# Linear attention in seven steps per head pair, and three modulation parts moved from the first layer's mixer to its MLP

## The chip, the cores and the metric

The kernel runs on one core of a Trainium2 chip. The metric is the device time of one execution in microseconds (us), as the median of several runs. TensorE multiplies matrices, VectorE and ScalarE do elementwise work, GpSimd some subtractions and clears, and SyncE issues most transfers.

## The reference

Two layers of a transformer-like block run over 512 latent and 256 context tokens of width 1024, all in float32. Every layer derives six modulation rows per stream, latent and context, from a conditioning vector:

```
mod_l = split(silu(c)     @ ada_w[layer] + ada_b[layer], 6)     # ada_w: 1024 x 6144
mod_c = split(silu(c_ctx) @ ada_w[layer] + ada_b[layer], 6)
u   = rmsnorm(x, g0) * (1 + mod[1]) + mod[0]
x   = x + mod[2] * rmsnorm(mix(u) @ w_out, g1)
x   = x + mod[5] * rmsnorm(relu(h @ w1)**2 @ w2, g3),   h = rmsnorm(x, g2) * (1 + mod[4]) + mod[3]
```

"Part (layer, i)" below is mod[i] of that layer. The mixer of layer 0 is a gated linear attention (8 heads, chunks of 64 tokens, forward and backward) beside a grouped-query softmax attention with rotary positions. The mixer of layer 1 is an mLSTM beside a retention. Only the latent stream leaves layer 1, so its parts 2 to 5 are wanted for the latent stream alone; all other parts are wanted for both streams.

## The kernel before, in words

Large float32 products are split into a rounded high and a low half (`split`, lines 196 to 198: ScalarE rounds, VectorE subtracts) and run as three matmuls (`mm3`, lines 488 to 490). The stages follow one another: startup with the first projection; the linear-attention stage; the softmax attention; the output projection; the first MLP; layer 1's mixer; its output projection; the second MLP.

**Order.** Within a stage Python generators cut the work into steps, and the strings of `PLAN` (line 133) say in which program order steps are taken. The framework puts in all semaphores, and its scheduler places the instructions on each engine by program order and its own estimates of when each can start. So a plan gives priority and the order in which buffers are handed out; a step's instructions can stand on an engine among those of other steps. On the engine itself, and in SyncE's queue, they run in order.

**Linear-attention stage** (`gla`, lines 805 to 963; driven at lines 1202 to 1208). One generator goes through the four head pairs one after the other, four steps a pair ("G", sixteen in all). A pair: gate products (L846), three ScalarE functions (L849 to L851), L852 on VectorE, cumulative sums on TensorE (L858), exponentials (L865), products with q and k (L874), transposes (L879), copies (L884, L886); then decays (L893) and chunk states (L908), their copies (L913), two scans (L919, L922); then scores (L935), mask (L938 to L944) and outputs (L954, L957); then a head norm. Its tiles E, Ei, Ek, lg, As and the scan's X have one buffer each. Among these steps stand "q", one token tile of the attention's query projection (24 matmuls, then rotary work that "l" advances), and "a", one step of `ada_steps` (lines 247 to 264). A step "a" loads two weight tiles of 128x1024 (512 KB) from `ada_w` and multiplies them, in fp32, with the conditioning of both streams on 32 columns: four 512-column products for two parts at once. Eight steps make a pair of parts, and `ada_finish` adds the bias and writes the rows to DRAM. The stage makes (0,2) with (0,3), (0,4) with (0,5), and (1,0) with (1,1): 24 steps, 48 tiles.

**The first MLP** (`mlp`, lines 585 to 792) goes through eight blocks of 512 hidden columns. A block has four hidden steps ("h") and seven products ("P") of one block against the hidden steps of the next. The sub-matrices of the second weight are subtracted on GpSimd (L638), and results are added into the sum on VectorE (L744). Every W1 and `ada_w` tile comes through one ring of three buffers (tag `raw`). Beside that "s" advances a side generator, `ada_part` (lines 293 to 317). It makes one part without matmuls: per step one 512 KB tile comes in, and VectorE multiplies its two halves by the conditioning and adds them up (L310 for the first half of a sum, L312 for the others), for the latent stream alone. After eight steps two fp32 products with a matrix of ones (L315) sum over the partitions, and `ada_rows` (lines 319 to 335) clears a tile on GpSimd (L324, L325), fetches the bias and writes the row out (L332, L333). The side generator makes (1,2) to (1,5) in the first MLP.

Of the kernel before, what the change touches and what calls it, by code (L numbers as in the profile page):

```python
# [8 lines left out]
F32 = mybir.dt.float32  # L9
# [3 lines left out]
ALU = mybir.AluOpType  # L13
# [109 lines left out]
def const_offsets():  # L123
# [11 lines left out]
    "gla": "GaGaGaqGaalGaaGalaqaaaGaGGlGlaaaqGaaaGaGlGlaqGGaaa",  # L135
    "att": "QQSSSSQSSSfSVSfSSSVSfSSSVfQSSSVSSVSSSVfQfVSSVVSfVSVQSSVSSVfVSVSSVSVSSVSVSVMSVSMVVSSVSSSVVSVMVVVVVVVM",
# [3 lines left out]
    "mlp": ["sPhPPshPPhsPPhsP", "PhPPhPPhPPhP"],  # L140
# [4 lines left out]
class Kern:  # L145
# [147 lines left out]
    def ada_part(self, layer, part, pool):  # L293

        nc = self.nc
        W = self.a["ada_w"][layer]
        c0 = part * 1024
        md = self.T(self.dram, [1, 1024])
        acc = [self.T(pool, [128, 512], F32, tag="sp", bufs=2) for _ in range(2)]
        for x in range(2):  # L300
            for kk in range(4):
# [4 lines left out]
                for k in range(2):  # L306
                    w = raw[:, k * 512:(k + 1) * 512]
                    c = self.sT[:, 2 * kk + k, 0:1]
                    if kk == 0 and k == 0:
                        nc.vector.tensor_scalar(out=acc[x], in0=w, scalar1=c, scalar2=None, op0=ALU.mult)  # L310
                    else:
                        nc.vector.scalar_tensor_tensor(out=acc[x], in0=w, scalar=c, in1=acc[x], op0=ALU.mult, op1=ALU.add)  # L312
        ps = self.pb()
        for x in range(2):
            nc.tensor.matmul(ps[32 * x:32 * x + 32, :], self.ones, acc[x], start=True, stop=True)  # L315
        self.ada_rows(layer, part, ps, [(0, 0), (512, 0)], md)
# [488 lines left out]
    def gla(self, ga, gqk, gv, lr, done):  # L805

        nc, C = self.nc, self.C0
        mm = nc.tensor.matmul
# [28 lines left out]
        nc.scalar.copy(lrT, pt[:, :768])  # L837

        X, XC = self.T(ga, [128, 708]), self.T(ga, [128, 256])
        nc.gpsimd.memset(X, 0.0)  # L840
        nc.gpsimd.memset(XC, 0.0)
        xc = XC.rearrange("p (e c) -> p e c", c=4)
        for p in range(4):
# [67 lines left out]
            for b in range(2):  # L911
                n = 6 - b
                nc.scalar.copy(U[:, :704].rearrange("p (e s) -> p s e", s=11)[:, b::2],  # L913
                               pu[:, b * 512:b * 512 + n * 64].rearrange("p (s e) -> p s e", s=n))

            for d in range(2):
# [27 lines left out]
            nc.vector.tensor_tensor(out=Av, in0=Av, in1=C["diag2"].unsqueeze(1).to_broadcast([128, 12, 64]), op=ALU.mult)  # L944
            po = self.pa()
# [211 lines left out]
    def layer0(self):  # L1157
# [6 lines left out]
        with self.pool("mx") as mx:  # L1164
# [11 lines left out]
            with self.pool("ga") as ga:  # L1176
# [21 lines left out]
                def ev2(t, ps):  # L1198
# [3 lines left out]
                ada = (x for layer, parts in ((0, (2, 3)), (0, (4, 5)), (1, (0, 1))) for x in self.ada_steps(layer, parts, self.po()))  # L1202
                gla = self.gla(ga, [gqk[:, p] for p in range(4)], [gv[:, p] for p in range(4)], lr,
                               lambda p: nc.sync.dma_start(out=on_d[p * 128:(p + 1) * 128, :], in_=gqk[:, p]))
                ops = {"G": lambda: next(gla), "q": lambda: next(qsteps), "a": lambda: next(ada, None), "l": later}
# [47 lines left out]
        with self.pool("xw", bufs=3) as xw, self.pool("h0") as h0:  # L1253
# [3 lines left out]
            with self.pool("p5") as p5, self.pool("ya") as yap:  # L1257
# [427 lines left out]
    def layer1(self):  # L1685
# [101 lines left out]
        with self.pool("xw1", bufs=3) as xw, self.pool("h1") as h1, self.pool("p7") as p7:  # L1787
# [20 lines left out]
            self.mlp(1, uT3, 512, (self.r2, self.r2), h1, acc, xw, ([(0, 256), (256, 512)], [(0, 512)]), done)  # L1808
# [42 lines left out]
```

## Time and profile before

| | |
|---|---|
| median of 3 runs | 1749.84 us (1747.56 to 1750.02) |
| the profiled execution | 1746.07 us |
| its span, first to last instruction | 1744.4 us |
| TensorE, VectorE, ScalarE, GpSimd busy | 95%, 65%, 45%, 15% |
| granted TensorE clock, mean | 0.981 of full speed |

The linear-attention stage lies at about 125 to 275 us of the span, the softmax attention up to 435, the output projection up to 522, the first MLP with its epilogue up to 1050, and the second MLP's steady part at 1430 to 1680. A row `L312 DVE ...` is line 312 of the kernel on VectorE (PE is TensorE, ACT ScalarE, POOL GpSimd, SPq SyncE's queue). All tiles have the name `x`.

### The profile page before, as it was taken

What the parts mean: (1) busy time and instruction counts of PE and PEld (TensorE: products, weight loads), DVE (VectorE), ACT (ScalarE), POOL (GpSimd) and SP (SyncE); (2) the same over time, 40 slices, a digit from 0 to 9 for tenths busy, and PEclk for the clock granted to TensorE, in tenths of its full rate; (3) what the DMA queues carried; (4) which work ended last, traced back from release to release, by engine and by line L of the source; (5) the groups of instructions that cost most, each with busy time, mean ns of one, the idle gap of its engine ahead of it and who ended that gap; (6) DMA issues with size and microseconds to landing.
All of it is one profiled execution on the core that took longest, in us unless ns stands there. A gap on an engine that the chain in (4) does not pass through costs nothing.

```text
span 1744.4 us, 25127 instructions
## 1 busy us (share of the span) xinstructions
PE 1660.3 (95%) x9795; PEld 1316.5 (75%) x9795; DVE 1131.3 (65%) x1678; ACT 791.5 (45%) x1392; POOL 264.3 (15%) x216
## 2 busy tenths in 40 slices
PE   7998999999999999999999999978998999999998
PEld 5775555755778888888888878757887788888876
DVE  5435456465678558657668693466786676777876
ACT  5335435464345434334333454635552355445443
POOL 0000020100002211121120000164011112223210
PEclk9999999999999999999999999988996999999999
DMA  9415666231654224224123552234545533333322
GB/s 289 129 52 178 202 205 223 72 91 37 205 169 128 90 61 155 74 83 157 62 90 118 176 192 64 84 104 130 161 132 164 181 98 108 110 108 99 107 86 84
DMA packets 174746, 220.67 MB, mean 127 GB/s; under 512 B 17450, under 2 KB 112742, under 8 KB 174628
## 3 DMA queue, kind: packets, MB, share of 16 engines
q1 hardware_dynamic: 169444, 201.24, 36.7%
q0 software_dynamic: 5184, 17.83, 3.0%
q8 instruction: 77, 1.26, 0.3%
q14 instruction: 41, 0.34, 0.1%
HBM read 193.74 MB, written 25.30 MB: 126 GB/s over the span
## 4 chain that ended last, share of the span: by engine, by line
PE 77%; DVE 9%; DMA 6%; ACT 4%; issue 3%; SPq 1%; POOL 0%; DVEq 0%; ACTq 0%; POOLq 0%
PE x L488 21%; PE x L489 21%; PE x L490 21%; DMA x<-in_ada_w_dram 2%; PE x L1116 2%; PE x L260 2%; DVE x L198 2%; PE x L1107 1%; PE x L1093 1%; DMA x<-x 1%; ACT x L197 1%; PE x L1542 1%; PE x L957 1%; PE x L435 1%; PE x L1681 1%
## 5 line engine op out<-in xcount | busy, mean ns | idle before, releaser
L488 PE MATMUL x<-x,x 128*128 128x512 f32 (+2 forms) x2042 | 763.3, 375 | 12.1 <-ACT x L197 3.4
L489 PE MATMUL x<-x,x 128*128 128x512 f32 (+2 forms) x2050 | 762.8, 373 | 7.1 <-DVE x L198 7.1
L490 PE MATMUL x<-x,x 128*128 128x512 f32 (+2 forms) x2050 | 761.1, 372 | 0.1
L198 DVE TENSOR_TENSOR x<-x,x 128x1024 fp32r<-128x1024 f32 (+4 forms) x373 | 395.5, 1079 | 216.5 <-ACT x L197 211.4
L197 ACT CAST x<-x 128x1024 fp32r<-128x1024 f32 (+4 forms) x373 | 332.7, 911 | 388.4 <-PE x L489 181.3
L488 PEld LDWEIGHTS x<-x,x 128*128 128x128 f32 x2042 | 387.4, 190 | 91.1 <-ACT x L197 9.0
L489 PEld LDWEIGHTS x<-x,x 128*128 128x128 f32 x2050 | 389.1, 190 | 75.7 <-DVE x L198 11.7
L490 PEld LDWEIGHTS x<-x,x 128*128 128x128 f32 x2050 | 388.9, 190 | 70.6 <-issue 6.3
L638 POOL TENSOR_TENSOR x<-x,x 128x1024 f32<-128x1024 f32 x56 | 145.5, 2599 | 546.3 <-DMA x<-in_mlp_w_dram 250.2
L744 DVE TENSOR_TENSOR x<-x,x 128x512 f32<-128x512 f32 x225 | 143.9, 680 | 12.3 <-PE x L490 11.2
L689 ACT ACTIVATE x<-x 128x512 f32<-128x512 f32 (+4 forms) x96 | 44.3, 477 | 91.2 <-PE x L490 91.2
L312 DVE SCALAR_TENSOR_TENSOR x<-x,x,x 128x512 f32<-128x512 f32 x56 | 53.1, 948 | 20.8 <-DMA x<-in_ada_w_dram 19.9
L260 PE MATMUL x<-x,x 128*32 128x512 f32 x192 | 45.6, 604 | 7.5 <-DMA x<-in_ada_w_dram 7.4
L690 ACT ACTIVATE x<-x 128x512 f32<-128x512 f32 (+4 forms) x96 | 48.0, 516 | 2.1
L1095 DVE TENSOR_REDUCE x<-x 128x1 f32<-128x768 f32 (+1 forms) x48 | 36.6, 775 | 18.9 <-PE x L1093 18.7
L1116 PE MATMUL x<-x,x 128*64 128x512 f32 x112 | 44.2, 618 | 1.0 <-ACT x L1110 0.7
L1096 ACT ACTIVATE x<-x,x 128x768 f32<-128x768 f32 (+1 forms) x48 | 36.3, 757 | 12.5 <-DVE x L1095 12.3
L1107 PEld LDWEIGHTS x<-x,x 128*128 128x128 f32 x224 | 24.5, 141 | 22.9 <-issue 21.1
L675 DVE TENSOR_TENSOR x<-x 128x768 f32<-128x768 f32 (+1 forms) x28 | 38.4, 1371 | 0.0
L1093 PE MATMUL x<-x,x 128*128 128x256 f32 (+1 forms) x160 | 36.7, 347 | 1.3 <-ACT x L1096 1.3
L799 DVE TENSOR_REDUCE x<-x 128x8 f32<-128x512 f32 (+1 forms) x19 | 14.3, 753 | 35.5 <-ACT x L797 35.4
L797 ACT ACTIVATE x<-x 128x512 f32<-128x512 f32 (+1 forms) x19 | 12.8, 673 | 47.6 <-PE x L957 25.8
(316 smaller groups left out, 1517.8 us busy)
## 6 DMA issues: line engine op xcount, KB each, us to landing
x<-in_mlp_w_dram SPq DMA_DIRECT2D x128, 512.0 KB
x<-in_ada_w_dram SPq DMA_DIRECT2D x96, 512.0 KB
x<-x SPq DMA_DIRECT2D x42, 512.0 KB
x<-x SPq DMA_DIRECT2D x50, 256.0 KB
x<-in_cd_w_in_dram SPq DMA_DIRECT2D x24, 512.0 KB
x<-x POOLq DMA_DIRECT2D x36, 256.0 KB, 3.1
x<-in_ab_w_in_dram SPq DMA_DIRECT2D x16, 512.0 KB
x<-x SPq DMA_DIRECT2D x20, 384.0 KB
```

Source lines behind the costliest of these rows:

```text
L197: self.nc.scalar.copy(hi, src)
L198: self.nc.vector.tensor_tensor(out=lo, in0=src, in1=hi.bitcast(F32), op=ALU.subtract)
L260: nc.tensor.matmul(ps[32 * g:32 * g + 32, :n], self.sT[:, k, :], rs[g], start=k == 0, stop=k == 7)
L312: nc.vector.scalar_tensor_tensor(out=acc[x], in0=w, scalar=c, in1=acc[x], op0=ALU.mult, op1=ALU.add)
L488: mm(out, st[0], mv[0], start=start, stop=False, skip_group_check=partial)
L489: mm(out, st[0], mv[1], start=False, stop=False, skip_group_check=partial)
L490: mm(out, st[1], mv[0], start=False, stop=stop, skip_group_check=partial)
L638: sub = lambda out, x, y: nc.gpsimd.tensor_tensor(out=out, in0=x, in1=y, op=ALU.subtract)
L690: nc.scalar.activation(out=hh[:, f, c0:c1], in_=h[:, c0:c1], func=AF.Square)
L744: nc.vector.tensor_tensor(out=dst, in0=dst, in1=acc[j], op=ALU.add)
L1093: mm(pS[:, s0:s1], qs[:, h * 128:(h + 1) * 128], kst[kv][i][:, s0:s1], start=i == 0, stop=i == 1)
L1116: mm(po[64 * kv:64 * kv + 64, :], av[:, kt * 128 + kv * 64:kt * 128 + kv * 64 + 64], PT[kv], start=kt == 0, stop=kt == nk - 1)
```

## The change

- **Linear attention.** The set-up common to all pairs becomes `gla_setup`. `gla` takes one pair `p`, and has three more yields (after the products with q and k, after the chunk states' copies, after the mask): seven steps a pair. Four generators stand side by side as "0" to "3" in the plan, which takes the later steps of one pair among the first of the next. X and XC become tiles with one buffer that each pair takes anew; only XC is still cleared.
- **Query tiles.** The plan of this stage takes all six "q" (four before) and twelve "l". One fill step "f" of the attention's plan stands elsewhere.
- **Modulation.** The stage keeps (0,2) with (0,3), and (0,4) alone: sixteen "a". With one part a step loads one tile and has four products of 256 columns.
- **The first MLP** makes (0,5), (1,0), (1,1), then (1,2), (1,3), (1,4). `ada_part` now makes a part for both streams (`ns` = 2) unless it is one of layer 1's later parts: four VectorE operations a tile, and a set of ones products and of rows for each half of 512 columns. The plan has six "s" a block (four before).
- **The second MLP** gets a side generator too, for (1,5), with two "s" a block; its ones and sums lie in the ring `t4` of seven tiles.

```
-    "gla": "GaGaGaqGaalGaaGalaqaaaGaGGlGlaaaqGaaaGaGlGlaqGGaaa",
+    "gla": "0a0q0l0a1la0q0l1a0l1aq1l2a1l1aq2l1a2l2a3ql2a2l3a2q3la3l3a3a3aa",
-    "mlp": ["sPhPPshPPhsPPhsP", "PhPPhPPhPPhP"],
+    "mlp": ["PshsPPshPPhssPPhsP", "PhPPshPPhPPhsP"],
...
-    def ada_part(self, layer, part, pool):
+    def ada_part(self, layer, part, new):
...
-        acc = [self.T(pool, [128, 512], F32, tag="sp", bufs=2) for _ in range(2)]
+        ns = 1 if layer == 1 and part > 1 else 2
+        md = self.T(self.dram, [2, 1024])
+        held = []
         for x in range(2):
+            acc = [new() for _ in range(ns)]
+            held += [(j, x, acc[j]) for j in range(ns)]
             for kk in range(4):
                 raw = self.T(self.w1, [128, 1024], F32, tag="raw", bufs=3)
...
                 yield
                 for k in range(2):
                     w = raw[:, k * 512:(k + 1) * 512]
-                    c = self.sT[:, 2 * kk + k, 0:1]
+                    for j in range(ns):
+                        c = self.sT[:, 2 * kk + k, j:j + 1]
+                        if kk == 0 and k == 0:
+                            nc.vector.tensor_scalar(out=acc[j], in0=w, scalar1=c, scalar2=None, op0=ALU.mult)
+                        else:
+                            nc.vector.scalar_tensor_tensor(out=acc[j], in0=w, scalar=c, in1=acc[j], op0=ALU.mult, op1=ALU.add)
+            if len(held) == 2:
+                ps = self.pb()
+                for i, (_, _, r) in enumerate(held):
+                    nc.tensor.matmul(ps[32 * i:32 * i + 32, :], self.ones, r, start=True, stop=True)
+                self.ada_rows(layer, part, ps, [(y * 512, j) for j, y, _ in held], md)
+                held = []
...
-    def gla(self, ga, gqk, gv, lr, done):
+    def gla_setup(self, ga, lr):
...
+        return wgr, lrT
+
+    def gla(self, ga, p, gqk, gv, sets, done):
...
+            yield
...
+            yield
+
+            X, XC = self.T(ga, [128, 708], tag="X", bufs=1), self.T(ga, [128, 256], tag="XC", bufs=1)
+            nc.gpsimd.memset(XC, 0.0)
...
+            yield
...
-                ada = (x for layer, parts in ((0, (2, 3)), (0, (4, 5)), (1, (0, 1))) for x in self.ada_steps(layer, parts, self.po()))
+                ada = (x for layer, parts in ((0, (2, 3)), (0, (4,))) for x in self.ada_steps(layer, parts, self.po()))
+                pair = [self.gla(ga, p, ...) for p in range(4)]
...
-                    for part in range(2, 6):
-                        yield from self.ada_part(1, part, p5)
+                    for layer, part in ((0, 5), (1, 0), (1, 1), (1, 2), (1, 3), (1, 4)):
+                        yield from self.ada_part(layer, part, lambda: self.T(p5, [128, 512], F32, tag="sp", bufs=2))
...
+            t4 = lambda: self.T(p7, [128, 1024], F32, tag="t4", bufs=7)
+            self.ones = t4()[:, :32]
+            self.mlp(1, ..., done, self.ada_part(1, 5, lambda: t4()[:, :512]))
```

## Rows read from the trace of the kernel before

**Rows 1.** The page: busy time and share by engine; the chain by engine.

```profile
PE 1660.3 (95%) x9795; PEld 1316.5 (75%) x9795; DVE 1131.3 (65%) x1678; ACT 791.5 (45%) x1392; POOL 264.3 (15%) x216
...
PE 77%; DVE 9%; DMA 6%; ACT 4%; issue 3%; SPq 1%; POOL 0%; DVEq 0%; ACTq 0%; POOLq 0%
```

**Rows 2.** Stretches of the span: busy us (instructions), granted clock, DMA share, GB/s.

```profile
core 0: us, PE busy (x) PEld busy (x) DVE busy (x) ACT busy (x) POOL busy (x), PEclk, DMA share, GB/s
124.90:275.00 150.10, 132.54 (x1765) 76.26 (x1764) 72.81 (x120) 66.67 (x117) 15.71 (x19) 0.99 0.61 200
275.00:435.00 160.00, 157.12 (x777) 99.67 (x776) 95.99 (x147) 87.85 (x185) 10.78 (x12) 1.00 0.28 92
522.00:541.00 19.00, 19.00 (x125) 17.37 (x124) 18.17 (x12) 8.53 (x13) 11.23 (x4) 1.00 0.47 140
522.00:780.00 258.00, 258.00 (x1351) 221.14 (x1350) 172.50 (x195) 110.00 (x164) 51.45 (x23) 1.00 0.32 97
780.00:985.00 205.00, 203.60 (x1041) 172.57 (x1039) 141.79 (x177) 76.98 (x108) 25.00 (x13) 1.00 0.38 120
985.00:1050.00 65.00, 63.03 (x295) 50.91 (x296) 59.67 (x130) 33.91 (x83) 2.21 (x4) 1.00 0.50 170
1430.00:1680.00 250.00, 249.41 (x1099) 205.70 (x1098) 188.99 (x218) 126.95 (x182) 62.92 (x24) 1.00 0.33 100
```

**Rows 3.** Groups by line, whole trace: busy us, mean ns | idle before, releasers.

```profile
L260 PE MATMUL x<-x,x 128*32 128x512 f32 x192 | 45.6, 604 | 7.5 <-DMA x<-in_ada_w_dram 7.4
...
L385 PE MATMUL x<-x,x 128*32 128x256 f32 x128 | 8.6, 385 | 0.0
...
L315 PE MATMUL x<-x,x 128*32 128x512 f32 x16 | 4.2, 604 | 0.0
```

**Rows 4.** Waits of TensorE, 124.9 to 275: us in total, times, longest.

```profile
PE x L260 <- DMA x<-in_ada_w_dram: 7.4, 7, 2.2
PE x L858 <- DVE x L852: 2.7, 2, 1.9
...
PE x L879 <- DVE x L874: 1.5, 1, 1.5
PE x L935 <- ACT x L913: 1.5, 1, 1.5
...
PE x L954 <- DVE x L944: 0.5, 1, 0.5
```

**Rows 5.** Line L846: ns min/median/max, first and last start us, form.

```profile
L846 PE MATMUL x<-x,x x24: 273/275/328, 132.7 to 233.2; 128*128 128x128 f32 x24
```

**Rows 6.** Groups of VectorE and GpSimd, 522 to 780.

```profile
L312 DVE SCALAR_TENSOR_TENSOR x<-x,x,x 128x512 f32<-128x512 f32 x30 | 33.7, 1122 | 11.3 <-DMA x<-in_ada_w_dram 10.8
...
L310 DVE TENSOR_SCALAR x<-x,x 128x512 f32<-128x512 f32 x4 | 1.9, 484 | 15.8 <-PE x L315 11.9 <-DMA x<-in_ada_w_dram 3.9
L333 DVE SCALAR_TENSOR_TENSOR x<-x 64x512 f32<-64x512 f32 x2 | 1.4, 676 | 0.0
L332 DVE TENSOR_TENSOR x<-x,x 64x512 f32<-64x512 f32 x2 | 1.3, 672 | 0.0
...
L638 POOL TENSOR_TENSOR x<-x,x 128x1024 f32<-128x1024 f32 x19 | 49.5, 2607 | 217.8 <-DMA x<-in_mlp_w_dram 87.9 <-DVE x L198 77.6 <-issue 51.8
```

**Rows 7.** Lines L312 and L744, whole trace: ns min/median/max, starts.

```profile
L312 DVE SCALAR_TENSOR_TENSOR x<-x,x,x x56: 736/752/2908, 521.5 to 949.8; 128x512 f32<-128x512 f32 x56
...
L744 DVE TENSOR_TENSOR x<-x,x x225: 669/680/689, 558.0 to 1693.3; 128x512 f32<-128x512 f32 x113
```

**Rows 8.** Timeline of VectorE: start us, us, instruction, count.

```profile
521.50 9.95 DVE L312 SCALAR_TENSOR_TENSOR x<-x,x,x 128x512 f32<-128x512 f32 x5
```

**Rows 9.** Waits of SyncE's queue, 522 to 780.

```profile
SPq L594 <- DVE x L312: 35.0, 11, 7.4
```

More of the change, by code (lines that the diff above doesn't have):

```diff
@@ L134 @@
     "start": "tttttt",
-    "gla": "GaGaGaqGaalGaaGalaqaaaGaGGlGlaaaqGaaaGaGlGlaqGGaaa",
-    "att": "QQSSSSQSSSfSVSfSSSVSfSSSVfQSSSVSSVSSSVfQfVSSVVSfVSVQSSVSSVfVSVSSVSVSSVSVSVMSVSMVVSSVSSSVVSVMVVVVVVVM",
+    "gla": "0a0q0l0a1la0q0l1a0l1aq1l2a1l1aq2l1a2l2a3ql2a2l3a2q3la3l3a3a3aa",
+    "att": "QQSSSSQSSSfSVSfSSSVSfSSSVfQSSSVSSVSSSVfQfVSSVVfVSSVQSSVSSVfVSVSSVSVSSVSVSVMSVSMVVSSVSSSVVSVMVVVVVVVM",
     "pre": 7,
@@ L307, in ada_part @@
                     w = raw[:, k * 512:(k + 1) * 512]
-                    c = self.sT[:, 2 * kk + k, 0:1]
[L309 to L316, printed above, removed]
+                    for j in range(ns):
[10 more added lines that the diff above has]
+                held = []
         self.mod[layer, part] = (md, 0)
@@ L802, in norm_heads @@
         return r
-    def gla(self, ga, gqk, gv, lr, done):
+    def gla_setup(self, ga, lr):
         nc, C = self.nc, self.C0
-        mm = nc.tensor.matmul
         wg = self.T(ga, [128, 512], F32, tag="As", bufs=1)
@@ L837, in gla @@
         nc.scalar.copy(lrT, pt[:, :768])
[L839 to L843, printed above, removed]
+        return wgr, lrT
+    def gla(self, ga, p, gqk, gv, sets, done):
+        nc, C = self.nc, self.C0
+        mm = nc.tensor.matmul
+        wgr, lrT = sets
+        for p in (p,):
             pz = self.pa()
@@ L914, in gla @@
                                pu[:, b * 512:b * 512 + n * 64].rearrange("p (s e) -> p s e", s=n))
+            yield
+            X, XC = self.T(ga, [128, 708], tag="X", bufs=1), self.T(ga, [128, 256], tag="XC", bufs=1)
+            xc = XC.rearrange("p (e c) -> p e c", c=4)
+            nc.gpsimd.memset(XC, 0.0)
             for d in range(2):
@@ L1201, in layer0 @@
                 qsteps = self.proj_steps(W, [(1568, 512)], uT, range(NT), ev2)
-                ada = (x for layer, parts in ((0, (2, 3)), (0, (4, 5)), (1, (0, 1))) for x in self.ada_steps(layer, parts, self.po()))
-                gla = self.gla(ga, [gqk[:, p] for p in range(4)], [gv[:, p] for p in range(4)], lr,
-                               lambda p: nc.sync.dma_start(out=on_d[p * 128:(p + 1) * 128, :], in_=gqk[:, p]))
-                ops = {"G": lambda: next(gla), "q": lambda: next(qsteps), "a": lambda: next(ada, None), "l": later}
+                ada = (x for layer, parts in ((0, (2, 3)), (0, (4,))) for x in self.ada_steps(layer, parts, self.po()))
+                sets = self.gla_setup(ga, lr)
+                pair = [self.gla(ga, p, [gqk[:, i] for i in range(4)], [gv[:, i] for i in range(4)], sets,
+                                 lambda p: nc.sync.dma_start(out=on_d[p * 128:(p + 1) * 128, :], in_=gqk[:, p])) for p in range(4)]
+                ops = {**{str(p): (lambda p=p: next(pair[p])) for p in range(4)}, "q": lambda: next(qsteps), "a": lambda: next(ada, None), "l": later}
                 for c in PLAN["gla"].replace(" ", ""):
@@ L1807, in done @@
                     self.post_halves(ss, xt, yg, self.out[0, i * 128:(i + 1) * 128, :])
-            self.mlp(1, uT3, 512, (self.r2, self.r2), h1, acc, xw, ([(0, 256), (256, 512)], [(0, 512)]), done)
+            t4 = lambda: self.T(p7, [128, 1024], F32, tag="t4", bufs=7)
+            self.ones = t4()[:, :32]
+            nc.vector.memset(self.ones, 1.0)
+            self.mlp(1, uT3, 512, (self.r2, self.r2), h1, acc, xw, ([(0, 256), (256, 512)], [(0, 512)]), done, self.ada_part(1, 5, lambda: t4()[:, :512]))
     def body(self):
```

1 line of the change is left out of this document (removed).

## The prediction

> **What bounds the kernel now.** I read the busy shares and the chain of waits first [rows 1]: TensorE is busy 95% of the span and 77% of the chain that ends last is TensorE, so an edit elsewhere counts only by what it does to TensorE's idle time. The profile's busy TensorE is not TensorE at its peak, so I then took the stretches that the change touches [rows 2]. The linear-attention stage (124.9 to 275) is the loose one: 132.5 of 150.1 us busy, 17.6 us idle. The attention after it has 2.9 us idle in 160, and the first MLP none at all from 522 to 780 and 1.4 from there to 985. In the MLP VectorE is the second engine: 172.5 of 258 us, then 141.8 of 205. In the last block with its epilogue (985 to 1050) it is busy 92%, and there TensorE already loses 2.0 us. So the change takes TensorE work out of a stage where TensorE sets the pace with gaps, and puts VectorE work where TensorE has no gaps and VectorE is the likeliest to make some.
>
> **Part 1: three modulation parts leave the linear-attention stage.** The stage holds 48 weight tiles of 512 KB, each with two 512-column fp32 products (four instructions), 45.6 us in all, 0.95 us a tile [rows 3]. After the change parts (0,2) and (0,3) keep 16 tiles, 15.2 us. Part (0,4) alone has 8 tiles of 256-column products, 64 instructions; the startup's products of just this shape cost 8.6 us for 128 [rows 3], so 4.3, and at most 7.6 if a tile stays at 0.95. I take 4.3, the same shape. Gain 45.6 - 19.5 = 26.1 us (22.8 to 26.1). One finish of eight small transfers goes too, off the path.
>
> Those tiles also made TensorE wait for their transfers, 7.4 us [rows 4]; half the transfers go and the stage moved 200 GB/s at 61% DMA [rows 2]. I take 5 off (0 to 7.4).
>
> **Part 2: seven steps per pair, two pairs interleaved.** The instructions per pair are the same; one clear of X goes, that of XC is made four times, on GpSimd, which is busy 15.7 of 150.1 us [rows 2]. What can change is the remaining 10.2 us of idle, of which VectorE and ScalarE links of the pair's own chain (L852, L874, L913, L944) make 6.2 [rows 4]. The scheduler already mixes the pairs with whatever is ready, so the finer hand order is priority, not a new freedom; and with 26 us of filler less, each link that is now covered is covered more thinly. The first and the last start of L846 stand 100.5 us apart over three pair distances and the last pair's six products, some 33 us a pair [rows 5], while TensorE's own work without modulation is at least 132.5 - 45.6, about 87 us for all four. I take 2 us gained (10 lost to 8 gained). Two more query tiles move in from the attention, and their 48 matmuls leave that stage, where TensorE is busy 98%: nothing in the sum; if they find gaps here that is a gain, which the 8 holds.
>
> Together 26.1 + 5 + 2 = 33.1 us off.
>
> **Part 3: what the first MLP gets.** A step of a part for both streams has four VectorE operations in place of two. Three such parts are 24 steps, 96 operations: 84 scalar_tensor_tensor and 12 tensor_scalar, and six row sets (L332 and L333) where one part had one. Part (1,5) goes to the second MLP.
>
> TensorE first: a set of two products with the ones costs 4.2 / 4 = 1.05 us [rows 3]. There were four sets; there will be 6 + 3 in the first MLP and 1 in the second: 6 more, 6.3 us, with nothing to hide them since TensorE has no gap there.
>
> VectorE: the 24 steps sit on 2 + 22 places of the plan, the hidden start and 3.7 of the blocks, so they fall into 522 to 780. That stretch now holds 33.7 + 1.9 + 1.4 + 1.3 = 38.3 us of the old part's work [rows 6]; without it 172.5 - 38.3 = 134.2. Added: 12 x 0.484 = 5.8, six sets x 1.35 = 8.1, and 84 scalar_tensor_tensor, whose price has two ends: alone 0.752 (the median [rows 7]), and 1.99 each where five ran beside GpSimd's subtractions [rows 8]. This stretch's own mean is 1.122 [rows 6], and I take that: 94.2. Sum 242.3 us of 258, 94%; by the low end 211 (82%), by the high end 315, which is 57 us too much.
>
> At 94% the mean fits, but VectorE works in order. A late step holds back the splits of the weights (L198) and the accumulation (L744) that frees a bank; it holds a buffer of the ring of three that the MLP's own weights use, and SyncE, in order too, already waits 35.0 us here to issue L594 behind L312 [rows 9]; GpSimd's clears (L324) queue before its subtractions. How much TensorE then loses no row shows for this stage; the nearest are 985 to 1050, at 92% with 3.0% lost, and 522 to 541, at 96% with nothing lost [rows 2]. 3% of 258 is 7.7; I take 8, and 1 for the lighter rest (780 to 985: 42 scalar_tensor_tensor in place of 56 - 30 = 26, two tensor_scalar and a set more, 156 of 205 [rows 2, 6, 7]). Together 9 (0 to 57).
>
> What the mean hides is GpSimd. L744 takes 669 to 689 ns whatever runs beside it, L312 from 736 to 2908 [rows 7]; the first reads one operand from PSUM, the second both from SBUF. The Trainium skill ("SBUF — State Buffer", Who interferes with whom) states this: a VectorE instruction with two SBUF inputs and a GpSimd one that reads SBUF exclude each other, and the later waits for the whole of the other. The trace agrees in kind. By it VectorE could lose at most GpSimd's 49.5 us of subtractions here [rows 6] to all its work: 134.2 + 63.2 + 13.9 + 49.5 = 260.8, 3 over the stretch where I take 9 with the rest; it speaks against the high end.
>
> **Part 4: the tail and the second MLP.** The six parts need 49 calls: 2 at the start, 36 in six blocks, 9 in the seventh, so the last two fall into the last block with its epilogue: 4 scalar_tensor_tensor and a set, 4.4 us on a VectorE that is busy 92% [rows 2]. I take 2 us (0 to 4.4). In the second MLP 14 scalar_tensor_tensor, two tensor_scalar and a set add 13 to 18 us to 189.0 of 250 [rows 2], about 80%; the products and splits cover it: 1 (0 to 5).
>
> **Sum.** -33.1 + 6.3 + 9 + 2 + 1 = -14.8 us. The profiled execution took 1746.07 us (span 1744.4), 3.8 below the median of the runs, 1749.84; the difference is applied to that median: 1735.0 us.
>
> **Rivals.**
>
> *All the new work finds room* (25%): TensorE lost nothing at 96% VectorE in 522 to 541. Then MLP 1, tail and second MLP 0, and the stage's waits go by 7.4 + 4: -26.1 - 11.4 + 6.3 + 1 = -30.2, 1719.6 us. Against it: in 985 to 1050 it did lose.
>
> *The pairs' own chain sets the stage* (13%): with less filler the pair distance of some 33 us barely shrinks, since E, Ei, Ek and lg have one buffer each and a pair starts only when the one before has run its scan. If half of the 33.1 comes, -16.5 + 18.3 = +1.8, 1751.6 us, no change that can be told. Against it: of 150.1 us TensorE waits for these links in only 6.2 [rows 4], and 87 us of its own work and 19.5 of modulation stay, with two query tiles besides.
>
> *VectorE becomes the bound of the first MLP* (17%, the other side): the place is 522 to 780, the price is what its queue exceeds 258 us. Without the MLP term the change gains 33.1 - 6.3 - 3 = 23.8, so it turns slower once VectorE needs over 281.8 us: (281.8 - 134.2 - 13.9) / 84 = 1.59 us per scalar_tensor_tensor, between the row's 1.12 and the 1.99 beside GpSimd. At 1.75 us: 295.1, 37.1 over, net +13, 1763 us.
>
> The change may also not do what it says in its first half: if the scheduler puts out the same interleaving, part 2 gives 0 and the rest stands, 1737; it is inside the forecast.
>
> **Numbers.** The forecast has 45%, its own range 1725 to 1746. Range for 8 in 10: 1717 to 1757, from the case with all the room to the middle of the slow one. A measurement of this kernel can tell about 0.2%, 3.5 us. Faster: 0.44 of the forecast, 0.25, and 0.02 of the chain case: 0.71. Within: 0.01 + 0.06 = 0.07. Slower: 0.05 of the chain case and 0.17: 0.22.
>
> **What would show it.** Right: the modulation products in the linear-attention stage near 19.5 us; the stage and the attention after it together some 33 us shorter; ten sets of ones products; VectorE near 94% in the MLP's first 258 us, with TensorE idle there of some 8 us behind L198 or L744. Wrong: TensorE idle of 24 us or more in the first MLP; a pair distance still near 33 us; a mean of L312 beyond 1.6 us; or a first MLP with no new idle at all.

## The result and the profile after

The changed kernel takes 1736.55 us (median of 4 runs, 1732.3 to 1740.32) against 1748.7 for the kernel before on the same chip: ratio 0.9932 [0.9905, 0.9959]. Forecast: 1735.0. Its profiled execution took 1732.3 us (span 1730.6), 13.8 less than that of before; the forecast was 14.8.

The page of the kernel after: busy time by engine, and the chain by engine.

```profile
PE 1646.4 (95%) x9755; PEld 1316.1 (76%) x9755; DVE 1224.8 (71%) x1783; ACT 790.7 (46%) x1392; POOL 274.1 (16%) x228
...
PE 65%; DVE 10%; DMA 4%; ACT 3%; issue 3%; SPq 1%; POOL 0%; DVEq 0%; ACTq 0%; POOLq 0%
```

Beside [rows 1], TensorE works 13.9 us less, VectorE 93.5 more. Stretches of the kernel after, with the columns of [rows 2]: us, then busy us (instructions) of each engine, granted clock, DMA share, GB/s. They are the linear-attention stage, the attention, the first 258 us of the first MLP's blocks, and the first two together.

```profile
125.60:262.40 136.80, 118.32 (x1763) 81.39 (x1761) 81.71 (x143) 71.79 (x132) 15.91 (x21) 0.96 0.44 144
262.40:411.50 149.10, 145.63 (x709) 92.66 (x709) 82.94 (x118) 79.13 (x167) 10.04 (x10) 0.98 0.25 78
501.70:759.70 258.00, 257.51 (x1340) 217.31 (x1340) 224.69 (x262) 108.34 (x161) 54.80 (x31) 1.00 0.36 111
125.60:411.50 285.90, 263.95 (x2471) 174.05 (x2469) 164.65 (x261) 150.92 (x299) 25.95 (x31) 0.97 0.34 110
```

Against [rows 2], the linear-attention stage is 13.3 us shorter and its TensorE idle has not fallen: 18.5 us after 17.6. The two together, up to the attention's last values product, take 285.9 us; before, from 124.9 to the same product at 433.9, they took 309.0. So the attention is 9.8 shorter. Of the 33.1 us forecast, 23.1 came. The clock column says a second thing. By the trace's clock records, from which it is made, 17.1 of these 286 us ran at the lower level of 1.2 GHz (0.97 granted); before it was 3.4 us.

In the MLP VectorE is busy 224.7 of 258 us (87%), where 94% was forecast, and TensorE is idle 0.5 us.

Groups by line of the kernel after: L260 in the stage, L321 over the whole trace, the others in 501.7 to 759.7.

```profile
L260 PE MATMUL x<-x,x 128*32 128x512 f32 (+1 forms) x128 | 19.9, 542 | 0.4 <-DMA x<-in_ada_w_dram 0.4
L321 PE MATMUL x<-x,x 128*32 128x512 f32 x40 | 10.5, 605 | 0.0
L317 DVE SCALAR_TENSOR_TENSOR x<-x,x,x 128x512 f32<-128x512 f32 x84 | 74.8, 945 | 5.0 <-DMA x<-in_ada_w_dram 5.0
L315 DVE TENSOR_SCALAR x<-x,x 128x512 f32<-128x512 f32 x12 | 10.6, 893 | 2.5 <-PE x L321 2.5
L645 POOL TENSOR_TENSOR x<-x,x 128x1024 f32<-128x1024 f32 x19 | 53.6, 2821 | 197.7 <-DVE x L198 98.3 <-DMA x<-in_mlp_w_dram 55.4 <-DVE x L339 27.2
```

L317 is the L312 of before, L321 its L315, L645 its L638. The modulation products fell from 45.6 us [rows 3] to 19.9, their waits for transfers from 7.4 [rows 4] to 0.4, near the forecast of 19.5 and better than the forecast of 2.4. What waits instead, TensorE from 125.5 to 262.4 (us in total, times, longest):

```profile
PE x L1061 <- DVE x L1056: 4.7, 2, 2.5
PE x L1107 <- DMA x<-x: 3.6, 1, 3.6
PE x L866 <- DVE x L860: 2.1, 2, 1.8
PE x L968 <- DVE x L957: 1.8, 2, 0.9
PE x L854 <- ACT x L922: 1.5, 1, 1.5
PE x L495 <- ACT x L197: 1.3, 1, 1.3
PE x L496 <- DVE x L198: 1.2, 1, 1.2
PE x L948 <- ACT x L922: 0.9, 1, 0.9
```

L1061 are the transposes of a query tile, behind its rotary subtraction on VectorE (L1056). L1107 is the attention's first scores product. L495 and L496 are the attention's filler (the gate projection), behind the splits of its weights. Of these 17.1 us, 10.8 belong to query tiles and to the handover to the attention, not to the pairs; the pairs' own links (L866, L968, L854, L948) make 6.3, after 6.2 [rows 4]. The handover on TensorE (start us, us, instruction, count, idle before):

```profile
254.55 0.49 PE L495 MATMUL x<-x,x 128*128 128x512 f32 x1 [1.28 <-ACT x L197]
256.28 0.50 PE L496 MATMUL x<-x,x 128*128 128x512 f32 x1 [1.23 <-DVE x L198]
256.61 0.40 PE L497 MATMUL x<-x,x 128*128 128x512 f32 x1
256.85 0.40 PE L495 MATMUL x<-x,x 128*128 128x512 f32 x1
...
262.38 1.19 PE L1107 MATMUL x<-x,x 128*128 128x256 f32 x4 [3.62 <-DMA x<-x]
263.37 0.63 PE L496 MATMUL x<-x,x 128*128 128x512 f32 x1
263.80 0.63 PE L497 MATMUL x<-x,x 128*128 128x512 f32 x1
```

and the query load that the scores wait for, on GpSimd's queue:

```profile
254.99 1.25 POOL L1072 DMA_DIRECT2D x<-x  x2 [9.77 <-DVE x L806]
```

The load goes into memory that the stage's pool gave up. It is issued behind a reduction of the last pair's head norm (L806), and the scores start 7.4 us later. The same two events in the kernel before (the issue, then the first scores on TensorE):

```profile
264.31 1.25 POOL L1058 DMA_DIRECT2D x<-x  x2 [10.46 <-DVE x L975]
```

```profile
275.01 0.72 PE L1093 MATMUL x<-x,x 128*128 128x256 f32 x4
```

There TensorE did query tiles and modulation products in the 10.7 us between the two, but for one wait of 2.2 us for a weight tile, and the scores found their load landed. Now the query tiles are used up. Products that start 0.24 us apart at 256.6 start 0.43 apart at 263.4: after the two waits of 1.2 us the granted clock fell to the lower level, from 257.3 for 10.2 us, with the wait of 3.62 inside that stretch. The other 6.9 us at that level lie at 240.2 and 247.1.

### The profile page after: what moved, and what is told of

It reads as the page before. It is cut to its first block, busy times and chain, and to the rows that moved or that the text cites. A ratio compares the mean times of both kernels' runs of the same rounds, so it can differ in the third digit from the quotient of the medians.

```text
span 1730.6 us, 25196 instructions
## 1 busy us (share of the span) xinstructions
PE 1646.4 (95%) x9755; PEld 1316.1 (76%) x9755; DVE 1224.8 (71%) x1783; ACT 790.7 (46%) x1392; POOL 274.1 (16%) x228
## 4 chain that ended last, share of the span: by engine, by line
PE 65%; DVE 10%; DMA 4%; ACT 3%; issue 3%; SPq 1%; POOL 0%; DVEq 0%; ACTq 0%; POOLq 0%
PE x L495 18%; PE x L497 18%; PE x L496 18%; DVE x L198 2%; PE x L1130 2%; DMA x<-x 2%; PE x L1121 1%; PE x L1107 1%; PE x L1556 1%; DMA x<-in_mlp_w_dram 1%; DMA x<-in_ada_w_dram 1%; ACT x L197 1%; DVE x L317 1%; PE x L1695 1%; PE x L442 1%
## 5 line engine op out<-in xcount | busy, mean ns | idle before, releaser
L495 PE MATMUL x<-x,x 128*128 128x512 f32 (+2 forms) x2042 | 766.3, 376 | 12.8 <-ACT x L197 7.3
L496 PE MATMUL x<-x,x 128*128 128x512 f32 (+2 forms) x2050 | 765.1, 374 | 8.7 <-DVE x L198 8.7
L198 DVE TENSOR_TENSOR x<-x,x 128x1024 fp32r<-128x1024 f32 (+4 forms) x373 | 403.7, 1102 | 164.1 <-ACT x L197 158.7
L197 ACT CAST x<-x 128x1024 fp32r<-128x1024 f32 (+4 forms) x373 | 332.4, 911 | 397.7 <-PE x L496 171.8
L495 PEld LDWEIGHTS x<-x,x 128*128 128x128 f32 x2042 | 388.4, 190 | 100.5 <-ACT x L197 17.4
L496 PEld LDWEIGHTS x<-x,x 128*128 128x128 f32 x2050 | 390.3, 190 | 78.4 <-DVE x L198 13.8
L497 PEld LDWEIGHTS x<-x,x 128*128 128x128 f32 x2050 | 389.9, 190 | 67.9 <-DVE x L198 2.7
L645 POOL TENSOR_TENSOR x<-x,x 128x1024 f32<-128x1024 f32 x56 | 150.6, 2689 | 498.9 <-DMA x<-in_mlp_w_dram 264.3
L751 DVE TENSOR_TENSOR x<-x,x 128x512 f32<-128x512 f32 x225 | 143.8, 679 | 11.5 <-PE x L497 10.6
L317 DVE SCALAR_TENSOR_TENSOR x<-x,x,x 128x512 f32<-128x512 f32 x140 | 127.1, 941 | 14.7 <-DMA x<-in_ada_w_dram 13.9
L1107 PE MATMUL x<-x,x 128*128 128x256 f32 (+1 forms) x160 | 38.9, 359 | 6.4 <-DMA x<-x 3.6
L1121 PEld LDWEIGHTS x<-x,x 128*128 128x128 f32 x224 | 24.7, 141 | 21.0 <-issue 20.3
L1107 PEld LDWEIGHTS x<-x,x 128*128 128x128 f32 x160 | 25.6, 197 | 13.9 <-ACT x L1110 7.6
L434 ACT ACTIVATE x<-x 128x1024 f32<-128x1024 f32 x16 | 17.0, 1061 | 39.3 <-DVE x L452 28.2
L1126 DVE COPY x<-x 128x512 f32<-128x512 f32 x28 | 19.3, 688 | 21.0 <-PE x L1121 20.7
L682 DVE TENSOR_TENSOR x<-x 128x768 f32<-128x768 f32 (+1 forms) x28 | 33.9, 1211 | 0.0
```

Source lines behind the costliest of these rows:

```text
L197: self.nc.scalar.copy(hi, src)
L198: self.nc.vector.tensor_tensor(out=lo, in0=src, in1=hi.bitcast(F32), op=ALU.subtract)
L317: nc.vector.scalar_tensor_tensor(out=acc[j], in0=w, scalar=c, in1=acc[j], op0=ALU.mult, op1=ALU.add)
L495: mm(out, st[0], mv[0], start=start, stop=False, skip_group_check=partial)
L496: mm(out, st[0], mv[1], start=False, stop=False, skip_group_check=partial)
L497: mm(out, st[1], mv[0], start=False, stop=stop, skip_group_check=partial)
```

## The experiments

Ratios are to the kernel before, timed in the same rounds; where two kernels were timed in different rounds, their ratios are compared.

**The changed kernel again**, as the base of the others.

> The changed kernel once more, as the measure for the other three on this chip: 0.990 to 0.996 of before in every theory.

1734.4 us, 0.9928 [0.9905, 0.9952]. The stage and the attention took 285.8 us, idle 21.8, 17.1 us at the lower clock: the picture holds in a second execution.

**The parts alone**: the modulation parts on VectorE as in the change, the linear attention as before.

```
(as in the kernel before)
"gla": "GaGaGaqGaalGaaGalaqaaaGaGGlGlaaaqGaaaGaGlGlaqGGaaa"   # takes (0,2) (0,3) (0,4) only
"mlp": ["PshsPPshPPhssPPhsP", "PhPPshPPhPPhsP"]             # as in the change
```

> The modulation parts move as in the change; linear attention stays one sequence of four steps a pair with four query tiles, as before. Theory A (the waits that grew from 10.2 to 18.1 us in the linear-attention stage come from the new order, above all from the two query tiles that no longer stand at its end): the stage's idle time falls to about 11 us, and the kernel takes 0.985 to 0.990 of before, some 7 us less than the changed kernel. Rival B (they come from the filler that is gone, whatever the order): idle time stays at 17 to 20 us, and the kernel is at 0.992 to 0.996 or, if the interleaving was worth something, above that. Both: no idle time of TensorE in the first MLP beyond 2 us.

1728.58 us, 0.9895 [0.9878, 0.9911]: the faster of the two, though the intervals overlap by a little. Its time came out as one theory had it, but its stage still has 19.3 us idle, as the other had it.

**The steps alone**: interleaved steps and six query tiles in the stage, all six parts' products kept there, and both MLPs as before.

```
-"gla": "0a0q0l0a1la0q0l1a0l1aq1l2a1l1aq2l1a2l2a3ql2a2l3a2q3la3l3a3a3aa"
+"gla": "0a0q0l0aa1la0q0l1aa0l1aq1l2aa1l1aq2l1aa2l2aa3ql2aa2l3a2q3laa3l3a3aa3aa"
-for layer, part in ((0, 5), (1, 0), (1, 1), (1, 2), (1, 3), (1, 4)):
+for layer, part in ((1, 2), (1, 3), (1, 4), (1, 5)):
```

> Seven steps a pair, interleaved, and six query tiles as in the change; all three pairs of modulation parts stay in the stage (24 steps a, eight of them doubled in the plan), and the MLPs are as before. Theory A: with all the filler the new order neither gains nor loses much in the middle and still loses at the handover to the attention: 0.997 to 1.002 of before. Rival B (the order covers waits well as long as there is filler): the 10 us of waits outside transfers halve, 0.995 to 0.997.

1749.75 us, 1.0009 [0.9994, 1.0024]. Alone the steps give nothing that can be told. The longest of TensorE's waits in this kernel from 125 to 285 names the place:

```profile
PE x L1107 <- DMA x<-x: 7.3, 1, 7.3
```

The first scores wait 7.3 us for their load. So it is late although all the modulation products are left in the stage.

**Four query tiles**: the changed kernel with the plan's last two "q" taken out, so that two tiles are left to the attention's first steps, as before the change.

```
-"gla": "0a0q0l0a1la0q0l1a0l1aq1l2a1l1aq2l1a2l2a3ql2a2l3a2q3la3l3a3a3aa"
+"gla": "0a0q0l0a1la0q0l1a0l1aq1l2a1l1aq2l1a2l2a3l2a2l3a23la3l3a3a3aa"
```

> The changed kernel with only the first four of the six query tiles in the stage's plan; the last two are then taken by the first fill steps of the attention, as before. Theory A: the two tiles (48 matmuls, some 11 us of TensorE) stand where TensorE waits 6.1 us for weights and for the first query load at the handover; the waits there fall below 2 us, and the time is 4 to 7 us under the changed kernel's. Rival B: the handover's wait is set by the chain of the last pair and the load behind it, the two tiles are already done by then or delay the gate projection by as much: within 2 us of the changed kernel.

1724.2 us, 0.9872 [0.9851, 0.9892], 10 us below the changed kernel in the same rounds. It beats both kernels. Its waits of TensorE from 124 to 254, and its stage and attention together:

```profile
PE x L948 <- issue: 2.8, 1, 2.8
PE x L1061 <- DVE x L1056: 2.2, 1, 2.2
```

```profile
125.00:403.00 278.00, 260.95 (x2470) 171.88 (x2468) 165.65 (x261) 151.11 (x299) 26.73 (x31) 0.99 0.35 113
```

Up to the first scores TensorE is idle for 12.7 us, where it was 18.5. The two query tiles now run while the load is under way (GpSimd's queue, then TensorE):

```profile
250.67 1.25 POOL L1072 DMA_DIRECT2D x<-x  x2 [11.57 <-DVE x L207]
```

```profile
255.22 0.71 PE L1107 MATMUL x<-x,x 128*128 128x256 f32 x4 [1.02 <-DMA x<-x]
255.77 0.40 PE L497 MATMUL x<-x,x 128*128 128x512 f32 x1
256.01 0.39 PE L495 MATMUL x<-x,x 128*128 128x512 f32 x1
```

The wait is 1.0 instead of 3.6, and the products after it stand at 0.24 us, full clock. But the load itself is faster too: the scores start 4.6 us after its issue, 7.4 in the changed kernel. While it was under way there, other transfers, on SyncE's queue, moved 0.86 MB, weights of the gate projection among them; here they moved 0.03 MB. Between issue and scores TensorE works 2.5 us there and 3.5 here. So of the idle time that is gone 2.8 us go with the shorter load, and only 1.0 with TensorE's having more to do. No run moved those weights alone, so that they make the load slow is not shown. From 309.0 to 278.0 is 31.0 us, nearly all of the 33.1 that the prediction gave the stage. **Run a second time** beside the last experiment, it kept its ratio:

> The version with four query tiles once more, as the measure for the next one on this chip: 0.985 to 0.990 of before.

1725.38 us, 0.9872 [0.9845, 0.9899].

**Steps, four tiles, all parts in the stage**: the interleaved order alone, without the two moved tiles.

```
(against the steps alone)
-"gla": "0a0q0l0aa1la0q0l1aa0l1aq1l2aa1l1aq2l1aa2l2aa3ql2aa2l3a2q3laa3l3a3aa3aa"
+"gla": "0a0q0l0aa1la0q0l1aa0l1aq1l2aa1l1aq2l1aa2l2aa3l2aa2l3a23laa3l3a3aa3aa"
```

> Seven steps a pair, interleaved, with four query tiles, all modulation parts still in the stage and the MLPs as before: the fourth corner beside before, the parts alone, and the changed kernel with four tiles. Theory A (what the order alone lost, 1.0009 of before with six tiles, is the handover without the two tiles): 0.995 to 0.998 of before, and the first scores wait for their load 2 us or less where the six-tile version waited 7.3. Rival B (the interleaved order itself loses while there is plenty of filler): 1.000 to 1.003, with the handover's wait gone all the same.

1746.92 us, 1.0009 [0.9992, 1.0025]. It fell out as the rival had it in time: with all the filler the interleaved order is worth nothing. Against both expectations the first scores still wait 3.6 us. Together, from one profile each (us; from the first transposes of the stage to the last values product; half clock is the time at the 1.2 GHz level):

```
                      parts    order        q   length  idle  half clock  1st scores  ratio
before                stage    in turn      4   309.0   20.4     3.4         -        1
parts alone           MLP      in turn      4   284.5   20.1    17.1        1.8       0.9895
steps, four tiles     stage    interleaved  4   312.4   19.7    20.5        3.6       1.0009
four tiles            MLP      interleaved  4   278.0   17.1     6.8        1.0       0.9872
steps alone           stage    interleaved  6   315.6   25.2    27.3        7.3       1.0009
the change            MLP      interleaved  6   285.9   21.9    17.1        3.6       0.9932
```

With half of the filler, interleaving gains 6.5 us of this stretch. The intervals of the two ratios overlap by a little, so the sign is likely rather than certain. With all the filler it costs 3.4, which is no more than two profiles of one order differ by (last section). The kernels with the interleaved order also have the moved fill step of the attention; no run tells it apart.

The two moved tiles cost 7.9 us with half of the filler, and that one is clear: in four profiles of each order (the kernels further down share the stage with one or the other) the stretch takes 285.6 to 288.9 us with six tiles and 277.2 to 281.7 with four, TensorE's idle is 21.3 to 21.9 and 14.9 to 17.0. With all the filler the tiles cost nothing that can be told: 1.0009 both ways. So moving the tiles costs only where the products are gone too.

**More work for VectorE.** Two kernels add scalar_tensor_tensor instructions to each step of the side generator, in place on the weight tile after its last use; their results go nowhere.

```
+ if layer == 0 or part < 5:
+     if k:                       # only in the first kernel; in the second, both halves
+         nc.vector.scalar_tensor_tensor(out=w, in0=w, scalar=c, in1=w, op0=ALU.mult, op1=ALU.max)
```

> The changed kernel with one more 128x512 scalar_tensor_tensor per side step of the first MLP (in place on the second half of the weight tile, after its last use; the result doesn't change). Per block of about 64 us that is 6 x 0.75 to 0.94 = 4.5 to 5.6 us on VectorE, whose fullest block of the changed kernel is busy 57.2: some 62.5, 97%. Theory A (VectorE costs nothing here until its queue is full): within 2 us of the changed kernel, no new wait of TensorE in the blocks. Rival B (lateness in order costs before it is full, as the forecast's 8 us at 94% had it): 5 us or more over the changed kernel, TensorE waiting behind L198 or L744 in the blocks.

1745.97 us, 0.9995 [0.9979, 1.0012]: 0.0067 or 11.6 us above the changed kernel. This is the rival that has the lateness begin before VectorE is full, though TensorE's waits are not behind L198 or L744, as the traces below show.

> Two more per side step, one for each half: 9 to 11.3 us a block, 66 to 68.5 us of VectorE in blocks of 64 us. Theory A: over the edge by 2 to 4.5 us in each of the 3.7 blocks with parts for both streams, nothing in the others: 6 to 17 us over the changed kernel, and the lines that TensorE waits for are VectorE's. Rival B: more than 17 us, since every block pays lateness on top. If neither shows (within 2 us), VectorE's busy time as the profile counts it overstates what it holds up.

1759.51 us, 1.0078 [1.0062, 1.0094]: 0.015 or some 26 us above, and so the rival again. The first four blocks of the MLP (each counted from the same activation), in the changed kernel, with one more, and with two more:

```profile
520.10:776.00 255.90, 255.41 (x1300) 213.48 (x1299) 220.57 (x263) 104.49 (x157) 50.81 (x26) 1.00 0.38 118
```

```profile
521.70:787.70 266.00, 259.07 (x1299) 215.26 (x1298) 235.15 (x286) 103.49 (x157) 53.59 (x26) 0.99 0.37 112
```

```profile
521.80:797.00 275.20, 263.13 (x1319) 217.37 (x1318) 251.19 (x305) 103.57 (x158) 56.66 (x28) 0.99 0.35 106
```

VectorE's work against the 256 us that TensorE needs is 86%, 92% and 98%. The changed kernel has 0.5 us of idle; the other two stretches are 10.1 and 19.3 us longer. In the last, 19 more matmuls fall into the stretch (1319 for 1300), some 4 us by their distance of 0.23; so about 15 are lost, 11.6 of them new idle. There TensorE waits 6.1 us for the splits on VectorE (L198) and 4.3 for one rounding (L197). In the kernel with one more, 6.4 of the 10.1 are new idle, most of it (5.1) in two waits, and a granted clock of 0.99 in place of 1.00 goes with the rest: a stretch of 3.4 us at the lower level in each of the two blocks that have these waits. One of them, read backwards. TensorE:

```profile
636.84 1.05 PE L324 MATMUL x<-x,x 128*32 128x512 f32 x4 [2.96 <-ACT x L699]
...
638.92 0.63 PE L498 MATMUL x<-x,x 128*128 128x512 f32 x1
639.35 0.63 PE L499 MATMUL x<-x,x 128*128 128x512 f32 x1
```

ScalarE, whose activation L699 stands behind the rounding of a weight tile that came late:

```profile
635.24 1.04 ACT L197 CAST x<-x 128x1024 fp32r<-128x1024 f32 x1 [16.16 <-DMA x<-in_mlp_w_dram]
636.19 0.59 ACT L699 ACTIVATE x<-x 128x512 f32<-128x512 f32 x1
```

SyncE's queue, which issued that tile (L604) at 631.0, and VectorE, which had then just let go of the buffer:

```profile
611.62 2.37 SPq L646 DMA_DIRECT2D x<-in_mlp_w_dram  x2
623.34 0.55 SPq L339 DMA_DIRECT2D x<-in_ada_b_dram  x2
...
631.00 0.39 SPq L604 DMA_DIRECT2D x<-in_mlp_w_dram  x1
```

```profile
619.20 2.88 DVE L317 SCALAR_TENSOR_TENSOR x<-x,x,x 128x512 f32<-128x512 f32 x1
...
630.23 0.74 DVE L320 SCALAR_TENSOR_TENSOR x<-x,x 128x512 f32<-128x512 f32 x1
636.32 1.23 DVE L198 TENSOR_TENSOR x<-x,x 128x1024 fp32r<-128x1024 f32 x1 [5.34 <-ACT x L197]
```

From 614.0 to 623.3 SyncE issues nothing: the bias load of a part (L339) stands at its head and waits for GpSimd's clear of the row tile, which ran at 622.8 behind another L320. The weight tile behind it then needs a buffer of the ring of three, which the last late L320 held until 631.0. VectorE itself stood idle for 5.34 us right after. The second of the two waits has the same chain but for its start: there the clear stood behind two of GpSimd's subtractions, and the tile was issued at 765.1, just after an L320, and rounded after 15.35 us of waiting. So in this kernel the loss is not a full VectorE; it is a queue in order and a ring of three behind a late one. The sums of SyncE's waits would not have told it: for L604 behind L320 they are 28.5 us over the four blocks, and 32.1 for the same wait (L601 behind L317) in the changed kernel, which loses nothing. The longest single waits differ: 11.1 for the clear after 8.0, and 16.2 of ScalarE for a weight tile after 9.7.

One rival stays open. The added instruction is itself the last reader of the ring's tile, so it adds work to VectorE and holds the buffer longer at once. A kernel that adds the work on another tile would tell the two apart; it was not run.

**Seven places a block**: the four-tile kernel with a seventh "s" in the plan of a block, to end the side work before the last block.

```
-"mlp": ["PshsPPshPPhssPPhsP", ...
+"mlp": ["PshsPPshsPPhssPPhsP", ...
```

> The changed kernel with four query tiles, and seven places for side steps per block of the first MLP instead of six, so that 53 calls are there before the last block where 49 are needed, and no VectorE step of a part falls into the last block with its epilogue. If those late steps cost what the epilogue grew by (33.4 to 34.9 us, and the stretch behind it 147.6 to 149.5), it is 1.5 to 3 us under the version with four tiles and six places. Rival: the epilogue grew for another reason (the order of layer 1's first products), within 1 us; or the denser VectorE work of the earlier blocks takes back as much.

1732.15 us, 0.9915 [0.9899, 0.9931], 0.0043 or 7.5 us above its base. The epilogue did shrink, 184.5 to 180.7, which speaks for a price of the tail (a second profile of the base has 182.4, so for some 2 to 4 us), but the stretch of the blocks ahead of it grew by 7.0 (454.0 to 461.0). In the first four VectorE has hardly more to do (222.7 us against 220.3), so it is not the load:

```profile
515.70:780.00 264.30, 257.81 (x1298) 213.31 (x1297) 222.70 (x274) 102.68 (x158) 52.46 (x28) 1.00 0.40 124
```

TensorE is idle 6.5 us there, 0.8 in the base. The longest wait (1.8 us) is put down to the row add of a part (L339), most of the rest to the rounding and splits of the weights. Which place of the new order brings them was not tried. In the profiles a further 3.7 us lie in the stage, of which below.

**Two more places in the seventh block only.**

```
-... if b < 6 else "PsPsPsPsPsPPhshshshs"
+... if b < 6 else "PsPsPsPsPsPsPshshshshs"
```

> The version with four query tiles, and two more side steps in the plan of the seventh block of the first MLP only (nine become eleven), so that all 49 calls are made before the last block with its epilogue, while the six blocks before keep six steps each. Theory A (late steps cost the epilogue some 3 to 4 us, as seven places per block had it: 184.5 to 180.7 us from the epilogue to layer 1; what that version lost was the denser work in the earlier blocks): that stretch falls to about 181 us, no new wait in the blocks, 2 to 4 us under the version with nine. Rival B (the seventh block has no room either): the block grows by what the epilogue gives back, within 1.5 us of it.

1727.01 us, 0.9884 [0.9855, 0.9912], which can't be told from the version with nine (0.9872). The epilogue fell by 1.9 us (182.4 to 180.5) and the stretch of the last blocks before it rose by 4.0 (135.9 to 139.9): no room there, which is the rival's sign, though the block lost twice what the epilogue gave back.

## Why the prediction was right, and which steps were not

**The forecast's kind and size held**: faster, 1736.55 for 1735.0. Two of its terms were wrong in opposite directions: the stage with the attention gave 10.0 us less than forecast, and the first MLP's blocks took 6.8 us where 9 and four sets of ones products, 4.2, were forecast. That the total still came out so close is luck. By the prediction's own signs, the modulation products and the ten sets came as named; the stage and the attention did not get 33 us shorter, VectorE stood at 87% and not near 94%, and "a first MLP with no new idle at all", a sign of being wrong, is what came.

**Part 1 held.** 19.9 us of products for 19.5, and 7.0 us of transfer waits gone for 5.

**Part 2 is the larger of the two mis-sized terms.** I gave the order +2 us of gain, in a range from 10 lost to 8 gained, and wrote of the moved query tiles "nothing in the sum". What it measured: 23.1 - 25.7 - 7.0 = -9.6 us, at the losing end of that range. The stage's idle behind anything but L260's transfers rose from 10.2 to 18.1 us; the two tiles cost 10 us of the kernel's time (0.9928 against 0.9872), of which the profiles show 7.9 in the stage and the attention: 4.8 of idle (the wait for the first query load and those of the query tiles' own transposes) and 3.0 us of busy time, with 10.3 us more at the lower clock. The step that failed is that I charged the tiles where they went and not where they left: the handover, which they had covered together with the modulation products. I also gave the first query load no price at all: from its issue to the scores it is 7.4 us, beside the gate projection's weights that now come earlier, and 4.6 with four tiles. The interleaving itself was right at about nothing, with all the filler. Here the pairs' chain did not set the pace: L854 answers to [rows 5],

```profile
L854 PE MATMUL x<-x,x x24: 223/275/328, 134.3 to 210.3; 128*128 128x128 f32 x24
```

first and last start 76.0 us apart, some 25 a pair where it was 33. With the pairs in turn and the same filler gone (the parts alone) the same two starts are 90.2 us apart, some 30 a pair. The starts of interleaved pairs are nearer by design, so the distance alone proves little; but TensorE's waits for the pairs' links have not grown either (6.3 us after 6.2), and 23.1 us came where the rival had 16.5. That speaks against the rival of the chain for this kernel.

**Part 3, ones products: held.** Ten sets; the first MLP as a whole is 6.8 us longer (474.7 to 481.5), and all of it is busy time: TensorE is idle 3.8 us in it before and after. Four of the new sets fall into it, 4.2 us; the fifth runs in the epilogue, the sixth in the second MLP. In the rest, 2.6 us, lies a stretch of 3.4 us at the lower clock, from 936.6, that the kernel before does not have.

**Part 3, VectorE: the price per scalar_tensor_tensor was too high.** 84 of them, as counted, cost 74.8 us, not 94.2. Five sets of rows took 9.0 us in this stretch, and the tensor_scalars 10.6 where I had 5.8. Sum 224.7 for 242.3. The spread shows why (ns min/median/max, first and last start):

```profile
L317 DVE SCALAR_TENSOR_TENSOR x<-x,x,x x140: 734/742/2924, 504.5 to 1523.5; 128x512 f32<-128x512 f32 x140
L751 DVE TENSOR_TENSOR x<-x,x x225: 670/679/689, 538.5 to 1679.5; 128x512 f32<-128x512 f32 x113
```

The median did not move. Only 19 of the 84 ran beside a GpSimd instruction at all, and eight of these took 2.88 to 2.91 us, each beside a subtraction (L645); no other took over 0.76. Before, six of the 30 were slow, 1.72 to 2.91 us. What they lose over the lone price is 84 x (0.945 - 0.742) = 17.1 us, before 30 x (1.122 - 0.752) = 11.1 [rows 6, 7]: the extra rose by half where the count rose 2.8 times, with 19 subtractions on GpSimd in both [rows 6]. My reading is that it is held down by the number of subtractions that there are to meet. The kernel with one more instruction fits: in its four blocks the 23 added ones took 17.1 us, 0.745 each, and L317 needed 66.2 for 65.4. No run changed the number of subtractions. I had multiplied a mean that held the extra by the new count. By 84 lone prices and the old extra it would have been 74.3.

**The lateness: nothing for 9.** In the changed kernel VectorE has 86% and the first MLP has no new idle, so the term was wrong here, because the load was put too high. Its kind shows in the kernel with one more instruction: 10.1 us at 92%, where 8 at 94% was forecast, by the path that the prediction named, the ring of three and SyncE's order, with the clears on GpSimd besides. It ends in ScalarE's rounding and L699, though, and not in L198 or L744. The rival "all the new work finds room" is thus right for the blocks of this kernel and would be wrong with one more instruction per step on the ring's tile; the rival of a bound VectorE needed 1.59 us per instruction and got 0.945.

The Trainium skill ("SBUF — State Buffer", Who interferes with whom) has a VectorE instruction with two SBUF inputs and a GpSimd instruction that reads SBUF block each other whole. The trace agrees: L317 up to 2924 ns, L751 with an operand in PSUM never over 689. The section also counts tensor_scalar among the operations that can meet GpSimd in this way; L315 fits that, at 893 ns, 484 before [rows 6]: of its 12, three took 1.8 to 2.6 us, each beside a subtraction on GpSimd, and nine 0.47 to 0.49.

**Part 4: held.** The epilogue came out 3.5 us longer (180.9 to 184.4) for 2 and the set of 1.05 in it, the second MLP 2.1 (324.6 to 326.7, to the end) for 2.05.

**What the sum leaves over.** Layer 1's mixer, which the change does not touch, took 5.9 us less in the profile. Its stretch in the kernel before, in the one after, and in the kernel of the steps with four tiles, whose parts are made as before:

```profile
1169.70:1419.80 250.10, 223.10 (x1555) 188.06 (x1555) 174.71 (x292) 114.43 (x241) 50.27 (x63) 0.92 0.48 151
```

```profile
1159.60:1403.90 244.30, 221.34 (x1555) 186.22 (x1555) 174.52 (x293) 114.53 (x241) 50.05 (x63) 0.93 0.48 154
```

```profile
1176.30:1420.90 244.60, 221.85 (x1555) 186.99 (x1555) 173.31 (x292) 114.57 (x241) 51.47 (x63) 0.93 0.49 154
```

The third has it too, with the same order of matmuls as the first. So it does not come from the change in the MLP; what goes with it is time at the lower clock, 41.0 us against 34.1 in both others, and 4 us of idle. Why it differs stays open, but it is hardly more than one order shows by itself: from the start of this mixer to the end of the span nine profiled kernels of this document have the same matmuls as the kernel after, and take 570.9 to 575.6 us; here the two are 571.0 and, before, 574.7. The profiled sum of the change is therefore -23.1 + 6.8 + 3.5 + 2.1 and 2.7 in startup and output projection, -8.0, and with the mixer's -5.9 it is, but for rounding, the 13.8 by which the spans differ; in the profile the forecast's closeness owes 6 us to something that it did not speak of.

## What to carry to other kernels

A filler that is moved forward leaves a hole where it stood: price the handover that it covered, and look for a load into reused memory that can only be issued there, and for the transfers that will run beside it. Of a mean that contains a few collided instructions, take the lone price for the new ones, and the collisions as a sum of their own. Work beside a saturated engine is not free until its engine is full: here nothing was lost at 86%, and 10 us at 92% when the added work also held a ring buffer longer, with a queue in order behind it; follow who frees the buffers, not the busy share alone. And when a total comes out as forecast, check its terms: here two of them were off by 6 and 10 us, in opposite directions.

## What the runs showed of the hardware that was not expected

A short wait of TensorE can cost twice: once as idle, and once as products at the 1.2 GHz level after it, 0.43 us apart in place of 0.24. In the MLP with one more instruction the wait of 2.96 us that ended at 636.8 was followed by 3.4 us at that level, from 638.2; the same four blocks of the changed kernel, without such waits, have none. Not every wait is followed so: the same blocks with seven places have 6.5 us of idle, 1.8 the longest wait, and no time at the lower level.

The granted clock is no fixed property of an order. The four-tile kernel and the one with seven places have the same matmuls in the same order through the stage and the attention, yet took 278.0 and 281.7 us, with 6.8 and 13.7 us at the lower level, one profile each (0.99 and 0.98 granted):

```profile
125.00:406.70 281.70, 264.73 (x2470) 174.71 (x2468) 165.65 (x261) 151.21 (x299) 26.75 (x31) 0.98 0.34 111
```

The two other profiles of that order have 277.2 and 279.6 us, with 6.8 and 13.7 at the lower level. A difference under some 4 us between two single profiles of such a stage is therefore not yet a finding; the 10 us of the two query tiles rest on the timed rounds, and on four profiles of either order that don't overlap.
